# Splitting the second mixer's weights one layer stage earlier and passing both parts through DRAM

## The chip, the cores and the metric

The kernel runs on one core of one Trainium2 chip. The metric is the device time of one execution in microseconds (us); of several executions the median is taken.

The core has a matrix engine (PE, with its weight load shown apart as PEld), a vector engine (DVE), an activation engine (ACT), a general engine (POOL) and a queue processor (SP). In this kernel SP issues every transfer between DRAM and the on-chip memory. Each engine works through its own list of instructions in order; an instruction that waits holds up everything behind it on its engine.

## The reference

Two layers run one after the other on 512 tokens of 1024 channels, in float32:

```
h = RMSNorm(x);  z = h @ W_in
a = sparse attention heads (the 128 best keys of each query, by an indexer)
s = S5 heads (a scan over tokens);  m = SSD heads (chunked)
x = x + concat(a, s, m) @ W_out
x = x + relu(RMSNorm(x) @ W_up)^2 @ W_down
```

The part of a layer up to `W_out` is called the mixer here, the last line the MLP. The indexer chooses keys, so products have to be good to about the last bit of float32.

## The kernel before

**Products.** A float32 matrix is held as two parts: `hi`, rounded to the format that PE multiplies fast (`F32R`), and `lo`, the rest. A product is three matmuls (hi·hi, hi·lo, lo·hi), in `mm3`, whose three calls are L436 to L438.

**Weights.** All weights come as slabs of at most 128 x 512 numbers (256 KB), in the order of use: `W_in` of a layer (40 slabs, of which the first 8, `kv`, have 332 columns), then `W_out` (16), then `W_up` and `W_down` (128). `Slabs.load` brings a slab into one of 3 buffers `wraw` (L159), `Slabs.split` makes `whi` on ACT (L171) and `wlo` on DVE (L172), each with 5 buffers. A new `whi` waits until PE has finished with the slab five before; a new `wraw` waits until DVE has split the slab three before. The program asks for slabs 3 ahead and splits them 1 ahead (`AHEAD`).

**Streams.** A mixer is made of several streams of work: the slices of `W_in` (order for the second layer: kv, xa, qi, z, u5, q, xb), the keys and index scores, the choice of keys (`isc`, `mx`: 16 rounds of MAX and MATCH_REPLACE for each of three blocks), attention, S5, SSD and the products with `W_out`. `merge` lays them side by side by costs and priorities, and a list scheduler then fixes each engine's order at build time. In the first MLP a stream `prepare` builds the second layer's S5 tables on POOL, with small transfers `M<-strip` on SP (L666).

**Around u5.** The S5 input slice `u5` needs the inverse root mean square of each token, `rsp`: three Newton steps on DVE (L299 to L305, tiles `rsi`, `rst`, `rsp`). Then ACT copies the product out of PE's accumulators into `usb` (L1186), which sets the accumulators free. The tile `cv` is the SSD convolution (L834 to L841), `cth` its tanh on ACT, `z` and `xb` other slices.

Of the kernel before, what the change touches and what calls it, by code (L numbers as in the profile page):

```python
# [22 lines left out]
NB = S // P          # token blocks  # L23
KC = D // P          # channel chunks of the trunk
# [8 lines left out]
T5 = 8               # tokens of one S5 chunk  # L33
C5 = S // T5         # S5 chunks
G5 = 16
GBUFS = {"g": 52, "t": 16}
BANKS = {"m": 4, "a": 4}    # PSUM banks: trunk, attention, S5 and SSD
EARLY = 2           # slabs loaded along with x
S5_ON_DVE = True
CONV_ON_ACT = False  # L40
# how the streams of work of a layer's mixers are laid side by side: the order of W_in's slices, the blocks whose
# selections run side by side, the parts of the out projection, which of S5 and SSD waits for the other, each
# stream's pace and delay, and the banks
# [41 lines left out]
WB = (3, 5)    # weight slabs in flight: as loaded, and split  # L85
OUTER = {"tok": True, "chan": True}    # products slab by slab
AHEAD = (3, 1)    # slabs requested and split ahead of the one in use

# columns of the packed per-partition parameters
# [18 lines left out]
# constants  # L108
# [8 lines left out]
# W_in slices: (first column, width), in the host's column order  # L117
# [16 lines left out]

class Slabs:
    """slabs of weight matrices in the order of their use: loaded and split into hi and lo parts some way ahead"""
# [9 lines left out]
    def turn(self, key):  # L146
        """whether the slabs before these have been used up"""
        return self.i == self.starts[key]

    def load(self, upto):  # L150
        for src in self.srcs[len(self.raw):upto]:
            net = self.net
            if len(self.raw) < EARLY:
                t = net.g(name="wraw0")
            else:
                t = net.wp.tile([P, 512], F32, tag="wraw", name=net.nm("wraw"), bufs=WB[0])
# [5 lines left out]
    def split(self, upto):  # L162
        upto = min(upto, len(self.srcs))
        self.load(upto)
        for raw in self.raw[len(self.hl):upto]:
            net = self.net
            nc = net.nc
# [13 lines left out]
    def take(self, n, tiles, outer):  # L181
        """the next n slabs for each of some tiles, as (tile, slab number, hi, lo): slab by slab if outer, else
        tile by tile, and then those to follow are split while the last tile uses these up"""
# [17 lines left out]
class Net:  # L201
    def __init__(self, ctx, tc, a, taps=None):
# [9 lines left out]
        self.sp = e(tc.tile_pool(name="sp", bufs=4))  # L212
        self.pp = {k: e(tc.tile_pool(name=f"p{k}", bufs=n, space=PSUM)) for k, n in BANKS.items()}
        self.uid = 0

# [9 lines left out]
    def h(self, shape=(P, 512), dt=F32, name="h"):  # L225
        """as g, for S5 and SSD"""
        return self.g(shape, dt, name, "h")

    def tt(self, shape=(P, 512), dt=F32, name="t"):
        """as g, for the matrices of S5"""  # L230
        return self.g(shape, dt, name, "t")

    def small(self, n, tag="g"):
        """[P, n] tiles for what one stretch of small instructions needs, cut from one slot"""
# [59 lines left out]
    def rsqrt(self, y, x, n, eng=None):  # L294
        """y = 1/sqrt(x), [P, n] small"""
# [11 lines left out]
    def stt(self, v, out, x, s, y, op0, op1):  # L307
        """out = (x op0 s) op1 y, [P, n] small; GpSimd takes two instructions for it"""
# [7 lines left out]
    def expacc(self, out, x, t, v):  # L316
        """out = exp(x) to about an ulp, [P, n] small"""
# [15 lines left out]
    def sincos(self, c, s, th, t, v):  # L333
        """c, s = cos(th), sin(th), [P, n] small"""
# [14 lines left out]
        self.stt(v, q, q, 1.0, r, ALU.add, ALU.mult)      # sin(th/2)  # L349
# [4 lines left out]
        # cos(th/2) = 1 + w  # L354
# [9 lines left out]
    def norm_chunk(self, c, squares=True):  # L364
        """hi and lo parts of x*g, and the sum of squares over channels (still per partition)"""
# [25 lines left out]
    def token_sums(self, acc, perm=False):  # L391
        """[P, 4]: mean square + eps per token; block b is tokens b*128 + m, or with perm 4m + 3-b"""
# [10 lines left out]
    def bcast_tokens(self, colv, k):  # L403
        """[P, 4] per-token columns -> psum tile [P, 512] with the token's value on every partition"""
# [6 lines left out]
    def add_slabs(self, l):  # L411
        """the weights of a layer, in the order of their use"""
# [9 lines left out]
        self.slabs.add(("in", l), [t for o in out for t in o])  # L422
# [5 lines left out]
        for part in PLAN[l]["out"]:  # L428
            self.slabs.add((part, l), square(a["w_out"][l], rows[part[0]][0], rows[part[-1]][1]))
# [3 lines left out]
    def mm3(self, p, lh, ll, rh, rl, first, last):  # L433
        """p += (lh+ll)^T (rh+rl), without the product of the two low parts (below float32's last bit)"""
# [5 lines left out]
    def gemm_tok(self, ps, xh, xl, slabs, sls):  # L440
        """token-major blocks: psum tile of block i [tok, n] = ps(i), tokens sls[i]; yields (cost, finished tile)"""
# [14 lines left out]
    def gemm_chan(self, ps, slabs, xh, xl):  # L456
        """channel-major tiles of 128 columns of a slice of 256: [chan, tok]; yields (cost, finished tile)"""
# [13 lines left out]
    def s5_small(self):  # L471
        """powers of the discretised state matrix and the input matrices, both layers"""
# [38 lines left out]
        # powers 0..8  # L511
# [17 lines left out]
        # X = (pr; pi), Y = (-pi; pr) on the two halves of the partitions  # L529
# [8 lines left out]
        # m8 and the rotation of one chunk, with the angle's sign turned on the lower half  # L538
# [4 lines left out]
        self.rot = []          # e^{+-i phi 2^k}  # L543
# [22 lines left out]
    def s5_tables(self, l, t):  # L566
        """the matrices of one layer's chunked recurrence, into t"""
# [29 lines left out]
        def outer(v, out, u, w, u2, w2, gs, d0, d1):  # L597
            """out[g, d, h] = u[g, h] w[g, d] + u2[g, h] w2[g, d]"""
# [935 lines left out]
```

## Time and profile before

| | |
|---|---|
| median of three runs | 1359.96 us (1359.14 to 1361.53) |
| span of the profiled execution | 1356.7 us; the median is 3.3 us longer, for what lies around the span |
| PE busy | 1247.9 us (92%), 5852 matmuls |
| DVE busy | 883.2 us (65%) |
| ACT busy | 564.6 us (42%) |
| POOL busy | 161.6 us (12%) |
| transfers | 103.7 MB, 76 GB/s over the span |

The execution has four stages: the first mixer (to about 329 us), the first MLP (to about 731), the second mixer (to about 1018) and the second MLP. The second mixer's first products begin some 20 us before 731, beside the end of the MLP. A matmul's listed duration overlaps that of the next: 128x512 products follow each other every 0.23 us though each is listed with 0.39.

### The profile page before, as it was taken

How to read it: one execution, taken by the hardware profiler on the slowest of the kernel's cores; microseconds unless marked ns; L12 is line 12 of the kernel's file. 1: busy time of each engine (PE TensorE's matmuls, PEld its weight loads, DVE VectorE, ACT ScalarE, POOL GpSimd, SP SyncE). 2: the span in 40 equal slices, each digit the busy share in tenths (PEclk: the TensorE clock that was granted, in tenths of full speed). 3: DMA queues.
4: the chain of work that ended last, by engine and by line, in shares of the span. 5: the costliest groups of instructions: out<-in, count | busy, mean ns of one | idle time of the engine just before them, and what ended most of it. 6: DMA issues, size and time to landing. Idle time of an engine off the chain costs nothing. (4 is left out here: it accounts for less than half of the span.)

```text
span 1356.7 us, 17071 instructions
## 1 busy us (share of the span) xinstructions
PE 1247.9 (92%) x5852; PEld 1013.6 (75%) x5852; DVE 883.2 (65%) x2044; ACT 564.6 (42%) x1160; POOL 161.6 (12%) x301
## 2 busy tenths in 40 slices
PE   6679966879999999999999998978999999999998
PEld 5667854647888877888888897755688888888887
DVE  6899799884844544444466779998575444445443
ACT  4346352563542332423444535656454233242331
POOL 2593268200000221000000000000000000000000
PEclk9789987899999999999999998989999999999999
DMA  6122120001233323323323312100123333333332
GB/s 193 47 78 71 25 68 11 32 1 47 86 95 100 94 83 94 101 96 99 94 84 89 100 31 53 63 16 16 35 83 102 95 99 94 101 94 101 93 108 86
DMA packets 102694, 103.74 MB, mean 76 GB/s; under 512 B 10960, under 2 KB 95696, under 8 KB 102608
## 3 DMA queue, kind: packets, MB, share of 16 engines
q1 hardware_dynamic: 102608, 102.66, 25.1%
q8 instruction: 46, 0.75, 0.2%
q14 instruction: 40, 0.33, 0.1%
HBM read 99.36 MB, written 2.10 MB: 75 GB/s over the span
## 5 line engine op out<-in xcount | busy, mean ns | idle before, releaser
L172 DVE TENSOR_TENSOR wlo<-wraw,whi 128x512 fp32r<-128x512 f32 (+1 forms) x368 | 253.8, 691 | 300.6 <-ACT whi L171 298.4
L171 ACT ACTIVATE whi<-wraw 128x512 fp32r<-128x512 f32 (+1 forms) x368 | 229.0, 624 | 498.5 <-PE pm L437 332.4
L436 PE MATMUL pm<-xh,whi 128*128 128x512 f32 x608 | 239.8, 395 | 2.7 <-ACT usb L1186 1.1
L437 PE MATMUL pm<-xl,whi 128*128 128x512 f32 x608 | 238.5, 393 | 0.0
L438 PE MATMUL pm<-xh,wlo 128*128 128x512 f32 x608 | 238.4, 393 | 0.0
L438 PE MATMUL pm<-uh,wlo 128*128 128x512 f32 x512 | 199.5, 390 | 1.2 <-DVE wlo L172 1.2
L437 PE MATMUL pm<-ul,whi 128*128 128x512 f32 x512 | 199.7, 390 | 0.0
L436 PE MATMUL pm<-uh,whi 128*128 128x512 f32 x512 | 199.6, 390 | 0.0
L436 PEld LDWEIGHTS pm<-xh,whi 128*128 128x128 f32 x608 | 115.2, 190 | 27.6 <-ACT q L1210 1.6
L438 PEld LDWEIGHTS pm<-xh,wlo 128*128 128x128 f32 x608 | 115.1, 189 | 24.4 <-issue 0.3
L437 PEld LDWEIGHTS pm<-xl,whi 128*128 128x128 f32 x608 | 115.3, 190 | 23.1 <-DVE xl L372 0.2
L438 PEld LDWEIGHTS pm<-uh,wlo 128*128 128x128 f32 x512 | 96.2, 188 | 21.7 <-DVE wlo L172 1.6
L436 PE MATMUL pm<-whi,xh 128*128 128x512 f32 (+2 forms) x240 | 94.1, 395 | 19.8 <-ACT xh L370 12.4
L437 PEld LDWEIGHTS pm<-ul,whi 128*128 128x128 f32 x512 | 96.2, 188 | 20.3 <-issue 0.4
L436 PEld LDWEIGHTS pm<-uh,whi 128*128 128x128 f32 x512 | 96.2, 188 | 19.9 <-issue 0.2
L437 PE MATMUL pm<-wlo,xh 128*128 128x512 f32 (+2 forms) x240 | 92.5, 386 | 2.3 <-DVE wlo L172 2.3
L438 PE MATMUL pm<-whi,xl 128*128 128x512 f32 (+2 forms) x240 | 92.2, 388 | 1.5 <-DVE xl L372 1.4
L436 PEld LDWEIGHTS pm<-whi,xh 128*128 128x128 f32 x240 | 55.9, 234 | 27.1 <-ACT xh L370 12.8
L437 PEld LDWEIGHTS pm<-wlo,xh 128*128 128x128 f32 x240 | 56.3, 235 | 7.6 <-DVE wlo L172 3.4
L438 PEld LDWEIGHTS pm<-whi,xl 128*128 128x128 f32 x240 | 55.7, 234 | 7.1 <-DVE xl L372 2.5
L1384 DVE SCALAR_TENSOR_TENSOR ur<-pm,ur 128x512 f32<-128x512 f32 x64 | 44.0, 687 | 25.5 <-ACT ur L1381 25.5
L1392 DVE TENSOR_TENSOR sq<-pm,r2b 128x512 f32<-128x512 f32 x64 | 44.2, 690 | 23.2 <-PE pm L438 23.2
(349 smaller groups left out, 1915.2 us busy)
## 6 DMA issues: line engine op xcount, KB each, us to landing
wraw<-in_w_up_dram SPq DMA_DIRECT2D x128, 256.0 KB, 2.7
wraw<-in_w_down_dram SPq DMA_DIRECT2D x128, 256.0 KB, 2.7
wraw<-in_w_in_dram SPq DMA_DIRECT2D x64, 256.0 KB, 2.7
wraw<-in_w_out_dram SPq DMA_DIRECT2D x32, 256.0 KB, 2.7
wraw<-in_w_in_dram SPq DMA_DIRECT2D x16, 166.0 KB, 2.3
x<-in_xT_dram SPq DMA_DIRECT2D x8, 256.0 KB, 5.9
out_dram<-x SPq DMA_DIRECT2D x8, 256.0 KB, 2.0
s5bc<-in_s5bc_dram SPq DMA_DIRECT2D x4, 256.0 KB, 4.7
```

The source lines that it names most:

```text
L171: nc.scalar.activation(hi, raw, AF.Copy)
L172: nc.vector.tensor_tensor(lo, raw, hi.bitcast(F32), ALU.subtract)
L436: nc.tensor.matmul(p, lh, rh, start=first, stop=False)
L437: nc.tensor.matmul(p, lh, rl, start=False, stop=False)
L438: nc.tensor.matmul(p, ll, rh, start=False, stop=last)
L1384: v.scalar_tensor_tensor(r, p, 0.0, r, ALU.max, ALU.mult)
L1392: v.tensor_tensor(t, d[1], rb, ALU.mult)
```

## The change

The 56 slabs of the second layer's `W_in` and `W_out` are no longer split by `Slabs.split`. A new stream `stage` runs beside the first MLP and the table stream: for each slab it loads the raw numbers (`sraw`), makes `shi` on ACT and `slo` on DVE, and stores both in DRAM (`st`). In the second mixer `Slabs.load` brings both parts straight into `whi` and `wlo`, by two transfers. The first layer and both MLPs are split as before.

```
+class Staged:
+    def __init__(self, src):
+        self.src, self.shape = src, src.shape
+        self.k, self.n = src.shape[0] // P, src.shape[1]
+        self.parts = None
...
     def load(self, upto):
         for src in self.srcs[len(self.raw):upto]:
             net = self.net
+            if isinstance(src, Staged):
+                hl = [net.wp.tile([P, 512], F32R, tag=t, name=net.nm(t), bufs=WB[1])[:, :src.k * src.n]
+                      for t in ("whi", "wlo")]
+                for t, d in zip(hl, src.parts):
+                    net.nc.sync.dma_start(t.bitcast(F32), d)
+                self.raw.append([t.rearrange("p (k n) -> p k n", k=src.k) for t in hl])
+                continue
...
     def split(self, upto):
...
+            if isinstance(raw, list):
+                self.hl.append(tuple(raw))
+                continue
...
+    def stage(self):
+        nc = self.nc
+        yield 6.0
+        for st in [t for t in self.slabs.srcs if isinstance(t, Staged)]:
+            w = st.k * st.n
+            raw, hi, lo = self.g(name="sraw")[:, :w], self.g(dt=F32R, name="shi")[:, :w], self.g(dt=F32R, name="slo")[:, :w]
+            nc.sync.dma_start(raw.rearrange("p (k n) -> p k n", k=st.k), st.src.rearrange("(k p) n -> p k n", p=P))
+            nc.scalar.activation(hi, raw, AF.Copy)
+            nc.vector.tensor_tensor(lo, raw, hi.bitcast(F32), ALU.subtract)
+            st.parts = [self.dp.tile([P, w], F32, tag=self.nm("st"), name=self.nm("st"), bufs=1) for _ in range(2)]
+            for d, t in zip(st.parts, (hi, lo)):
+                nc.sync.dma_start(d, t.bitcast(F32))
+            yield 5.3
...
             if l + 1 < L:
                 streams.append((self.prepare(l + 1), 0.0))
+                streams.append((self.stage(), 0.0))
```

Line numbers in the rows of the changed kernel are its own: L1437 is the store of `stage`, L167 the load of a staged part, L1099 and L1100 are MAX and MATCH_REPLACE, L321 to L326 the steps of `rsp`, L860 and L864 belong to `cv`.

On DVE, in the second mixer, where the steps of `rsp` for the slice u5 stand (`isc` of 128x256 belongs to the key choice of the first block that has one, `isc<-irl` to the last block's index scores). Before:

```order
L299 TENSOR_SCALAR rsi_1845_7697<-ms_7694 128x4
L172 TENSOR_TENSOR wlo_7744<-wraw_7644,whi_7743 128x512
L837 SCALAR_TENSOR_TENSOR cv_7561<-xa_7112,hconvw,cv_7561 128x509
L300 TENSOR_SCALAR rsp_7696<-rsi_1845_7697 128x4
L172 TENSOR_TENSOR wlo_7973<-wraw_7677,whi_7972 128x512
L303 TENSOR_TENSOR rst_1846_7700<-rsp_7696 128x4
L841 SCALAR_TENSOR_TENSOR cv_7561<-cth_7566,cv_7561 128x512
L1066 SCALAR_TENSOR_TENSOR isc_7426<-irl_7572,wd_6683,isc_7426 128x512
L304 SCALAR_TENSOR_TENSOR rst_1846_7700<-rst_1846_7700,ms_7694 128x4
L172 TENSOR_TENSOR wlo_7997<-wraw_7741,whi_7996 128x512
L1066 SCALAR_TENSOR_TENSOR isc_7426<-irl_7614,wd_6683,isc_7426 128x512
L305 SCALAR_TENSOR_TENSOR rsp_7696<-rst_1846_7700,rsp_7696 128x4
```

The same place after the change:

```order
L320 TENSOR_SCALAR rsi_2210_8205<-ms_8202 128x4
L1100 MATCH_REPLACE isc_7790<-mx_2266_8514,isc_7790 128x256
L860 SCALAR_TENSOR_TENSOR cv_8075<-xa_7652,hconvw,cv_8075 128x509
L321 TENSOR_SCALAR rsp_8204<-rsi_2210_8205 128x4
L1099 MAX mx_2269_8533<-isc_7790 128x8
L324 TENSOR_TENSOR rst_2211_8208<-rsp_8204 128x4
L1099 MAX mx_2434_9146<-isc_7870 128x8
L864 SCALAR_TENSOR_TENSOR cv_8075<-cth_8080,cv_8075 128x512
L1089 SCALAR_TENSOR_TENSOR isc_7950<-irl_8086,wd_7247,isc_7950 128x512
L325 SCALAR_TENSOR_TENSOR rst_2211_8208<-rst_2211_8208,ms_8202 128x4
L1100 MATCH_REPLACE isc_7790<-mx_2269_8533,isc_7790 128x256
L1089 SCALAR_TENSOR_TENSOR isc_7950<-irl_8126,wd_7247,isc_7950 128x512
```

The four `wlo` between the first and the last step of `rsp` are gone (the fourth stood just below the rows shown), and rounds of the key choice, which stood later before, have moved up between the steps.

On SP, in the first MLP, loads of its own weights before the change:

```order
L159 DMA wraw_4166<-in_w_down_dram 128x2x256
L159 DMA wraw_4190<-in_w_down_dram 128x2x256
L159 DMA wraw_4210<-in_w_up_dram 128x2x256
L159 DMA wraw_4228<-in_w_up_dram 128x2x256
L159 DMA wraw_4246<-in_w_up_dram 128x2x256
```

A place of the first MLP after the change:

```order
L1432 DMA sraw_4142<-in_w_in_dram 128x2x256
L176 DMA wraw_4252<-in_w_down_dram 128x2x256
L176 DMA wraw_4270<-in_w_down_dram 128x2x256
L1437 DMA st_4148<-shi_4143 128x512
L1437 DMA st_4149<-slo_4144 128x512
L1432 DMA sraw_4188<-in_w_in_dram 128x2x256
L176 DMA wraw_4298<-in_w_down_dram 128x2x256
L176 DMA wraw_4322<-in_w_down_dram 128x2x256
```

After every two loads of the MLP's own weights SP now has two stores, which wait for ACT and DVE, and one load for the next staged slab.

On SP, where the second mixer's weights begin to be loaded, after the change (before, each slab is one row `wraw<-in_w_in_dram` there):

```order
L176 DMA wraw_7148<-in_w_down_dram 128x2x256
L167 DMA whi_7168<-st_3656 128x332
L167 DMA wlo_7169<-st_3657 128x332
L176 DMA wraw_9920<-in_w_up_dram 128x2x256
L176 DMA wraw_9952<-in_w_up_dram 128x2x256
L167 DMA whi_7188<-st_3717 128x332
L167 DMA wlo_7189<-st_3718 128x332
L176 DMA wraw_9984<-in_w_up_dram 128x2x256
```

Each slab is now two rows, and the first three slabs of the second MLP, whose `wraw` buffers the mixer no longer uses, are loaded some 290 us before they are needed.

## Rows read from the trace of the kernel before

**Rows 1.** Stages: us; PE, PEld, DVE, ACT, POOL busy (count); clock; DMA share; GB/s.

```profile
329.00:731.00 402.00, 398.86 (x1828) 331.44 (x1827) 213.62 (x333) 148.46 (x252) 21.51 (x34) 1.00 0.31 95
731.00:1018.00 287.00, 257.74 (x1294) 203.13 (x1293) 229.56 (x658) 152.37 (x359) 0.52 (x1) 0.95 0.17 50
```

**Rows 2.** Groups of instructions, 725 to 1020 us: the splits of the second mixer.

```profile
L172 DVE TENSOR_TENSOR wlo<-wraw,whi 128x512 fp32r<-128x512 f32 x56 | 38.2, 686 | 11.5 <-ACT whi L171 10.9 <-PE pm L438 0.2
...
L171 ACT ACTIVATE whi<-wraw 128x512 fp32r<-128x512 f32 x56 | 35.3, 632 | 57.7 <-PE pm L437 23.6 <-PE pm L438 22.8 <-issue 6.0
```

**Rows 3.** PE's waits, 715 to 830 us (us in total, times, longest).

```profile
PE pm L436 <- ACT usb L1186: 5.2, 1, 5.2
PE pm L436 <- ACT whi L171: 1.4, 2, 0.7
...
PE pm L437 <- DVE wlo L172: 0.6, 2, 0.4
```

**Rows 4.** DVE in order of time (start, us; idle before and releaser).

```profile
802.47 0.16 DVE L299 TENSOR_SCALAR rsi<-ms 128x4 int32<-128x4 int32 x1
805.15 0.69 DVE L172 TENSOR_TENSOR wlo<-wraw,whi 128x512 fp32r<-128x512 f32 x1 [2.52 <-ACT whi L171]
805.76 0.74 DVE L837 SCALAR_TENSOR_TENSOR cv<-xa,hconvw,cv 128x509 f32<-128x509 f32 x1
...
810.04 0.69 DVE L841 SCALAR_TENSOR_TENSOR cv<-cth,cv 128x512 f32<-128x512 f32 x1 [2.55 <-ACT cth L839]
...
814.14 0.42 DVE L1076 MAX8 mx<-isc 128x8 f32<-128x256 f32 x1
...
816.47 0.14 DVE L305 SCALAR_TENSOR_TENSOR rsp<-rst,rsp 128x4 f32<-128x4 f32 x1
```

**Rows 5.** ACT in order of time, 795 to 830 us.

```profile
808.86 0.63 ACT L171 ACTIVATE whi<-wraw 128x512 fp32r<-128x512 f32 x1 [2.16 <-PE pm L438]
809.40 0.61 ACT L839 ACTIVATE cth<-cv 128x512 f32<-128x512 f32 x1
```

**Rows 6.** PE in order of time: the last u5 product, and the next.

```profile
811.70 0.40 PE L438 MATMUL pm<-whi,xl 128*128 128x256 f32 x1
817.32 0.80 PE L436 MATMUL pm<-whi,xh 128*128 128x512 f32 x1 [5.23 <-ACT usb L1186]
```

**Rows 7.** Stretches of 4 us around that gap (PE busy; granted clock).

```profile
800.00:804.00 4.00, 4.00 (x17) 0.80 0.00 0
...
816.00:820.00 4.00, 2.68 (x9) 0.50 0.10 35
820.00:824.00 4.00, 4.00 (x26) 0.64 0.00 0
```

**Rows 8.** The chain of waits that ended last, splits on it from 829 us.

```profile
848.05 0.69 DVE wlo L172
...
872.02 0.52 ACT whi L171
...
885.83 0.60 DVE wlo L172
```

**Rows 9.** SP in order of time, 470 to 560 us, in the first MLP.

```profile
470.93 29.59 SPq L159 DMA_DIRECT2D wraw<-in_w_down_dram  x11
502.24 16.37 SPq L666 DMA_DIRECT2D M<-strip  x24
```

**Rows 10.** PE's waits for DVE, 330 to 735 us (total, times, longest).

```profile
PE pm L438 <- DVE wlo L172: 1.2, 1, 1.2
```

**Rows 11.** Transfers: issue on SP (ns), then issues by kind with time to landing.

```profile
L159 SPq DMA_DIRECT2D wraw<-in_w_up_dram x128: 367/368/957, 333.9 to 1288.1; - x128
```

**Rows 12.** The page's transfers by kind (KB each, median us to landing).

```profile
wraw<-in_w_in_dram SPq DMA_DIRECT2D x64, 256.0 KB, 2.7
...
out_dram<-x SPq DMA_DIRECT2D x8, 256.0 KB, 2.0
```

**Rows 13.** Two microseconds of the opening load of x (DMA share; GB/s).

```profile
8.00:10.00 2.00, 0.16 (x1) 0.16 (x1) 0.68 (x2) 1.30 (x3) 2.00 (x9) 1.00 1.05 399
```

More of the change, by code (lines that the diff above doesn't have):

```diff
@@ L212, in __init__ @@
         self.sp = e(tc.tile_pool(name="sp", bufs=4))
+        self.dp = e(tc.tile_pool(name="dp", bufs=2, space=bass.MemoryType.DRAM))
         self.pp = {k: e(tc.tile_pool(name=f"p{k}", bufs=n, space=PSUM)) for k, n in BANKS.items()}
@@ L421, in add_slabs @@
             out[:2] = [[t for j in range(4) for t in (kv[2 * j], kv[2 * j + 1], x[j])]]
-        self.slabs.add(("in", l), [t for o in out for t in o])
+        out = [t for o in out for t in o]
+        self.slabs.add(("in", l), [Staged(t) for t in out] if l else out)
         def square(w, r0, r1):
@@ L428, in add_slabs @@
         for part in PLAN[l]["out"]:
-            self.slabs.add((part, l), square(a["w_out"][l], rows[part[0]][0], rows[part[-1]][1]))
+            out = square(a["w_out"][l], rows[part[0]][0], rows[part[-1]][1])
+            self.slabs.add((part, l), [Staged(t) for t in out] if l else out)
         self.slabs.add(("mlp", l), [t for q in range(0, FF, D)
```

## The prediction

> **What bounds the kernel now.** I read the busy times by stage first [rows 1]. In the first MLP PE is busy 398.86 of 402 us while DVE and ACT are busy 213.62 and 148.46 and the transfers take .31 of their engines: PE bounds it and all others have room. In the second mixer PE is busy 257.74 of 287 us and DVE 229.56, so about 29 us of the stage are not PE's, and neither is DVE the bound by its sum alone. What a lighter DVE is worth there depends on where PE stands still. I therefore looked at the groups for the work that leaves [rows 2], at PE's waits [rows 3], then at DVE, ACT and PE in order of time round the longest of these waits [rows 4 to 6] with the clock beside it [rows 7], and at the chain of waits for the rest [rows 8]. For what is added I read SP in the first MLP [rows 9], what PE lost there [rows 10], and the prices of transfers [rows 11 to 13].
>
> **What leaves the second mixer.** 56 `wlo` on DVE (38.2 us busy; one is listed with 0.69 but the next begins 0.61 us behind it, at 805.76 after 805.15 [rows 4]) and 56 `whi` on ACT (35.3 us) [rows 2]. That is 17% of DVE's busy time in the stage, but only what stands between two pieces of PE work is a gain:
>
> *Before u5.* Between 715 and 830 us PE waited directly for splits only four times: `whi` 1.4 us and `wlo` 0.6 us [rows 3]. Both go: **−2.0**.
>
> *The u5 gap.* PE starts its last u5 product at 811.70 and its next at 817.32, having stood 5.23 us for ACT's `usb` [rows 6]; that is the 5.2 of [rows 3]. `usb` needs the last `rsp` step, which starts on DVE at 816.47 and ends at 816.6; the first step starts at 802.47 [rows 4]. So the chain lasts 14.1 us. In it lie 2.52 us in which DVE waited for a `whi`, 2.55 in which it waited for `cth`, and four `wlo` of about 0.60, 2.4 together. The wait for `cth` falls too: ACT ran `cth` at 809.40 only because the `whi` at 808.86 ahead of it had stood 2.16 us until PE freed its buffer [rows 5]. Against that, the change puts ten rounds of MAX and MATCH_REPLACE between the steps, where five stood before (the order of the program, counted to the last step); one takes about 0.4 us [rows 4], so +2.0. The chain becomes 14.1 − 2.5 − 2.5 − 2.4 + 2.0 = 8.7 us and ends near 811.2; with the 0.7 us from there to PE's start, PE may go on at 811.9, and its last product before ends at 812.1. Nearly all of the 5.2 would go; I take **−4.5**, because a transfer or `cv` may be late next. The ends: −1 if the waits for ACT stay in another form, −5.2 if all goes.
>
> *The clock.* Around the gap the granted clock was .80 at 800 to 804 while PE was busy all 4 us, then .50 at 816 to 820 with PE busy 2.68, and .64 at 820 to 824 with PE busy 4.00 [rows 7]; .50 is the 1.2 GHz level, 1.00 that of 2.4 GHz. At the level of 2.4 GHz the busy time of the last two stretches would have needed 2.68 × .5 + 4.00 × .64 = 3.9 us instead of 6.68: 2.8 us lost. If PE doesn't stand, this loss may go. But ACT's copies out of PE's accumulators pace the same stretch, and the clock was already low at 800 before any gap; between 0 and −2.8 I take **−0.5**.
>
> The Trainium skill, "TensorE: Matmul & The Clock Gate", Part 1, says that the clock is gated by PE's recent activity, so that standing idle drops it to the lower level. The half clock right behind the 5.23 us agrees [rows 6, 7]; the .80 beside a busy PE does not follow from it. By that rule alone the whole 2.8 us would come back, by the rows I count a part.
>
> *After 829 us* the chain that ended last runs for a part over DVE, and six `wlo` lie on it, from 848.05 to 885.83, with 3.74 us in all, and two `whi` of 0.52 [rows 8], 4.8 us. A piece that leaves the chain gives back its length only until the next path ends last, and rounds of the key choice can fill its place only where they were not due anyway. I count four fifths: **−3.9**, with bounds 0 and −4.8. A later stand of PE, near 905 us, has no split ahead of it, and I leave it.
>
> **What is added to the first MLP.** The same 56 splits: 35 us for ACT (148 busy of 402) and 38 us for DVE (214 of 402) [rows 1, 2]. Both would be at most 63% busy, behind a PE that is at 99%; the splits of the MLP run a few slabs ahead, limited by their five buffers, so half a microsecond on either engine is taken from that lead. Cost 0; without the lead it would be one `wlo`, 0.6, per staged slab, 34 us.
>
> SP has 168 more instructions there, 56 loads and 112 stores, at .37 us [rows 11] 62 us of issuing. That is no load on SP by itself; the question is what they hold up. A store waits for `shi` or `slo`, and behind it stand the MLP's own loads. How sensitive PE is to a held SP can be read: 24 strips of M held SP for 16.37 us, with no weight load among them [rows 9], and PE's whole wait for `wlo` in the stage was 1.2 us [rows 10]. The buffers therefore cover some 14 us. Ahead of a pair of stores stand two `wraw` loads, which themselves wait for buffers, so ACT and DVE have about 5.4 us (two slabs at SP's 2.7 [rows 9]) for the load of 2.7 us [rows 12] and the two splits. Round the strips two stores and a load are added to a cover that is just used up: I take **+2.0** in the whole stage, from 0 to +4.
>
> The transfers: 14 MB read and 28 MB written in about 297 us are 141 GB/s beside the 95 of [rows 1], 236 in all; at 8 to 10 us the trace has 399 [rows 13]. It fits.
>
> **What is added to the second mixer.** Two loads for one, 28 MB instead of 14. PE takes a slab of `qi` in some 2.07 us (nine spans of 0.23), 0.52 MB in that time being 250 GB/s, under the 399 [rows 13]. The load is now issued when PE frees the fifth buffer back; then four slabs, over 7 us, remain for a landing of 2.7 us [rows 12], or some 4 with two issues and other traffic. This removes the engine from the path, but it also makes SP wait for PE where it waited for DVE. I take **+1.0**, from 0 to +4. Behind a waiting load stand only small parameter loads and the next parts.
>
> **Sum.** −2.0 − 4.5 − 0.5 − 3.9 + 2.0 + 1.0 = −7.9 us. From the span of 1356.7 that is 1348.8; the median of the runs is 3.3 us over the span, so 1352.1. The terms' ends on one side or the other give 1347 to 1358 as this case's own range.
>
> **Rivals.**
>
> *SP is held in the first MLP (slower).* If the pace does not hide the staged slab, SP's cycle is its issue .37, the landing 2.7, `shi` .63, a store .37, `slo` .69, a store .37 and two loads .74 [rows 2, 11, 12], together 5.9 us. SP's own pace is 29.59 us for eleven loads [rows 9], 2.7 a slab and 5.4 for the two. Over 56 staged slabs 0.5 us each are 28; some 14 are covered, 14 stay, and with the mixer's gains of 8 kept the time is about 1366. It decides from the point at which a staged slab holds SP longer than PE needs for two slabs of the MLP. Against it: the load is put two paced loads ahead of its stores, which takes the 2.7 us out of the sum.
>
> By the Trainium skill, "DMA: Bandwidth & Descriptors", Anatomy of one DMA, a transfer's wait for a semaphore is served by the issuing sequencer before dispatch, so waiting stores do hold the loads behind them; and a write to DRAM has the heaviest receipt. The first agrees with [rows 9]; no row shows the second, the stores of the output landing in 2.0 us against 2.7 for loads [rows 12].
>
> *The gains are eaten (same).* The gap of u5 is filled by the added rounds of the key choice, or its place is taken by `cv` and ACT; the pieces on the chain come back at 905 us, and +3 to +5 of transfers remain: −2.0 − 1 − 1 + 4 = 0, 1360.
>
> *A larger gain.* DVE's rounds of the key choice are what the later part of the mixer waits for, and all 38 us that leave let them end earlier; with the whole clock loss back and no cost in the first MLP it would be −2.0 − 5.2 − 2.8 − 4.8 = −14.8, about 1345, and the prefetched slabs at the start of the second MLP can add a little.
>
> That the change doesn't do what it says is out: the order has none of the `wlo` in the second mixer, and SP's list is 224 longer, four for each of 56 slabs.
>
> **Chances.** The forecast .58; larger gain .12; eaten .16; SP held .14. Within 0.2%, 2.7 us, which is about what a measurement of this kernel can tell from no change, lie the eaten case and the upper edge of the forecast; a part of the slow case ends there too. Faster .69, same .17, slower .14. The range leaves out the slow case above 1363 and a bit of the large gain below 1343.
>
> **What would show it.** Right: no PE wait for `usb` over 1 us near 812; the mixer's span shorter by about 10 us and the first MLP's within 3 us of before; `sraw` landing in about 3 us. Wrong: PE waits of MLP for `wlo` or `whi` spread over all of the first MLP (SP held), or PE waits in the mixer for DMA `whi` or `wlo` (loads late); or PE's gap at u5 as before with another releaser.

## The result, and the profile after

The changed kernel takes 1371.3 us (median of 1366.5 to 1374.3), the kernel before 1359.6 in the same comparison: 0.81% slower, a ratio of 1.0081 with a 95% interval of 1.0058 to 1.0104. I had forecast 1352.1.

The stage windows of the changed kernel, which answer to [rows 1], show the first MLP with more work and a PE that now stands still:

```profile
329.00:731.00 402.00, 383.43 (x1685) 311.29 (x1684) 226.68 (x353) 167.64 (x288) 17.50 (x29) 0.98 0.62 194
731.00:1018.00 287.00, 262.86 (x1368) 211.87 (x1367) 207.95 (x622) 125.96 (x314) 0.52 (x1) 0.97 0.32 101
```

PE has 1685 matmuls in the same 402 us instead of 1828: the stage is not over at 731. Its end can be read from the last residual sum of the first MLP on DVE (`x<-x,sq`), and the end of the second mixer from its last one (`x<-x,pm`). In order of time on DVE, kernel before:

```profile
716.92 0.69 DVE L1393 TENSOR_TENSOR x<-x,sq 128x512 f32<-128x512 f32 x1
...
1012.77 0.69 DVE L1354 TENSOR_TENSOR x<-x,pm 128x512 f32<-128x512 f32 x1 [2.00 <-PE pm L438]
```

The same two rows of the changed kernel:

```profile
738.80 0.69 DVE L1416 TENSOR_TENSOR x<-x,sq 128x512 f32<-128x512 f32 x1
...
1024.73 0.69 DVE L1377 TENSOR_TENSOR x<-x,pm 128x512 f32<-128x512 f32 x1 [2.25 <-PE pm L461]
```

From one row to the other the second mixer takes 285.9 instead of 295.9 us, 9.9 less. But it begins 21.9 us later. Taken from the first mixer's last sum (end at 357.3 before, 354.8 after), the first MLP takes 384.7 instead of 360.3 us: 24.4 more. By stages the profiled executions differ by −2.5, +24.4, −9.9 and +0.1, in sum by the 12.0 us between the spans of 1356.7 and 1368.7. The −2.5 lies in the first mixer, which the change doesn't touch (see the end).

The two windows of the first MLP hold the same 1608 matmuls, before and after:

```profile
357.34:717.61 360.27, 357.13 (x1608) 294.57 (x1607) 184.02 (x278) 128.62 (x219) 21.51 (x34) 1.00 0.31 95
354.79:739.49 384.70, 366.13 (x1608) 297.15 (x1607) 212.15 (x329) 156.54 (x270) 17.50 (x29) 0.98 0.64 201
```

PE stands 18.6 us instead of 3.1, which is 15.4 more, and is busy 9.0 us longer for the same products, at a granted clock of .98 instead of 1.00.

PE's waits in the first MLP (330 to 740 us; us in total, times, longest), to be laid beside [rows 10]:

```profile
PE pm L459 <- DVE ur L1407: 12.9, 6, 4.8
PE s5st L676 <- POOL CA L629: 3.2, 2, 1.6
PE pm L459 <- DVE sq L1415: 2.5, 4, 1.4
```

No wait for `whi` or `wlo` is left: the MLP's weights are there in time. PE waits for `ur` and `sq`, the copies that take a finished product out of its accumulators, 15.4 us in all. Behind the two longest waits the granted clock falls as well (stretches of 20 us; the last three numbers are clock, DMA share and GB/s):

```profile
580.00:600.00 20.00, 14.46 (x56) 10.91 (x55) 10.09 (x16) 9.40 (x16) 0.00 (x0) 0.90 0.65 208
600.00:620.00 20.00, 20.00 (x83) 16.14 (x83) 8.61 (x14) 5.25 (x9) 0.00 (x0) 0.93 0.55 174
680.00:700.00 20.00, 14.35 (x51) 10.56 (x50) 9.74 (x15) 9.04 (x16) 0.00 (x0) 0.87 0.67 215
```

What happens at such a wait is seen round 592 us, on three engines. SP in order of time:

```profile
591.40 0.34 SPq L1437 DMA_DIRECT2D st<-slo  x1
591.79 0.45 SPq L1432 DMA_DIRECT2D sraw<-in_w_in_dram  x1
```

ACT:

```profile
592.13 0.63 ACT L191 ACTIVATE whi<-wraw 128x512 fp32r<-128x512 f32 x1 [1.57 <-issue]
595.10 0.63 ACT L1433 ACTIVATE shi<-sraw 128x512 fp32r<-128x512 f32 x1 [2.34 <-DMA sraw<-in_w_in_dram]
595.64 0.58 ACT L1404 ACTIVATE ur<-pm 128x512 f32<-128x512 f32 x1
```

PE:

```profile
591.88 0.39 PE L461 MATMUL pm<-uh,wlo 128*128 128x512 f32 x1
597.11 1.88 PE L459 MATMUL pm<-uh,whi 128*128 128x512 f32 x3 [4.84 <-DVE ur L1407]
```

PE finishes a product at 592.3 and needs the copies that empty its accumulators: ACT's `ur`, and behind it DVE's `ur`, which the row names. ACT could do its own at 592.8, but its next instruction is `shi`, which waits 2.34 us for the raw staged slab. That slab was requested only at 591.79, because its load stands in SP's list behind the store of the slab before, and this store waited for `slo`. So a staged slab goes round a ring: load, `shi`, `slo`, store, next load. And ACT's list has `shi` straight ahead of the copy that PE waits for. All six waits for `ur` lie behind a `shi` that had stood for `sraw`, for 0.9 to 4.7 us. DVE's list has the same form: the `sq` of the longest such wait (1.41 us, before 552.67) stands directly behind a `slo` that had waited 1.38 us for its `shi`.

ACT's own waits from 357 to 740 us show what it stood for (us in total, times, longest):

```profile
ACT shi L1433 <- DMA sraw<-in_w_out_dram: 43.9, 14, 4.7
ACT shi L1433 <- DMA sraw<-in_w_in_dram: 38.9, 30, 2.7
ACT whi L191 <- DMA wraw<-in_w_up_dram: 7.3, 8, 1.7
```

It stood 82.8 us for staged slabs and under 8 for the MLP's own, less than the 12.4 us of the kernel before (357 to 718 us). SP's list did not hold the MLP's own loads back to any effect here.

The ring's period is read from the tile view of `sraw` (min/median/max ns on SP, first and last issue):

```profile
L1432 SPq DMA_DIRECT2D sraw<-in_w_out_dram x16: 399/442/503, 610.6 to 706.5; - x16
```

15 steps in 95.9 us are 6.4 us each, PE's own waits included. Where nothing is held, as in e1_ahead below, the same 15 steps take 82.2 us, 5.5 each: that is the pace at which the stage was laid beside the MLP. Early in the stage the changed kernel keeps it too: 23 steps from 368.3 to 496.4 us, 5.6 each. Then the strips hold SP, and the next `sraw` is issued at 517.5.

In the second mixer, PE's waits (735 to 1030 us) have neither `usb` nor `whi` nor `wlo` in them, where [rows 3] had all three. The largest that are left:

```profile
PE ssds L906 <- DVE CT L871: 4.8, 1, 4.8
PE pTp L1136 <- ACT pe L1128: 3.0, 3, 2.4
PE kTp L1043 <- ACT khi L1037: 2.9, 1, 2.9
```

### The profile page after: what moved, and what is told of

It reads as the page before. It is cut to its first block, busy times and chain, and to the rows that moved or that the text cites. A ratio compares the mean times of both kernels' runs of the same rounds, so it can differ in the third digit from the quotient of the medians.

```text
span 1368.7 us, 17369 instructions
## 1 busy us (share of the span) xinstructions
PE 1249.4 (91%) x5852; PEld 1010.4 (74%) x5852; DVE 884.6 (65%) x2044; ACT 563.0 (41%) x1160; POOL 161.3 (12%) x301
## 4 chain that ended last, share of the span: by engine, by line
PE 70%; DVE 16%; ACT 6%; DMA 4%; issue 2%; SPq 0%; POOL 0%; ACTq 0%; DVEq 0%
PE pm L459 20%; PE pm L460 20%; PE pm L461 20%; PE po L1141 2%; DMA sraw<-in_w_in_dram 2%; DMA sraw<-in_w_out_dram 2%; PE pTp L1136 1%; DVE isc L1100 1%; DVE mx L1099 1%; DVE wlo L192 1%; ACT pe L1121 1%; DVE pe L1120 1%; DVE isc L1089 1%; DVE cv L860 1%; PE hTp L1059 1%
## 5 line engine op out<-in xcount | busy, mean ns | idle before, releaser
L192 DVE TENSOR_TENSOR wlo<-wraw,whi 128x512 fp32r<-128x512 f32 (+1 forms) x312 | 217.4, 700 | 224.6 <-ACT whi L191 222.8
L191 ACT ACTIVATE whi<-wraw 128x512 fp32r<-128x512 f32 (+1 forms) x312 | 194.3, 625 | 358.8 <-PE pm L460 239.8
L459 PE MATMUL pm<-uh,whi 128*128 128x512 f32 x512 | 201.9, 396 | 11.7 <-DVE ur L1407 11.2
L1434 DVE TENSOR_TENSOR slo<-sraw,shi 128x512 fp32r<-128x512 f32 (+1 forms) x56 | 37.3, 666 | 78.0 <-ACT shi L1433 74.8
L1433 ACT ACTIVATE shi<-sraw 128x512 fp32r<-128x512 f32 (+1 forms) x56 | 34.0, 608 | 82.9 <-DMA sraw<-in_w_out_dram 43.9
```

What stands on the lines that cost most here:

```text
L191: nc.scalar.activation(hi, raw, AF.Copy)
L192: nc.vector.tensor_tensor(lo, raw, hi.bitcast(F32), ALU.subtract)
L459: nc.tensor.matmul(p, lh, rh, start=first, stop=False)
L1433: nc.scalar.activation(hi, raw, AF.Copy)
L1434: nc.vector.tensor_tensor(lo, raw, hi.bitcast(F32), ALU.subtract)
```

## The experiments

The theory after this reading, called RING or ORDER in the expectations: the loss comes of the ring, whose period under load is about as long as the stage's step. Rivals: the traffic as such (VOLUME, LOAD or TRAFFIC), and the 73 us of added work on ACT and DVE (WORK). All experiments start from the changed kernel.

**e1_ahead.** The raw slab of the next step is requested before the present one is split.

```
+        raws = [fetch(sts[0])]
+        for n, st in enumerate(sts):
+            if n + 1 < len(sts):
+                raws.append(fetch(sts[n + 1]))
             ... (split raws[n], store)
```

> The raw slab of the next stage step is requested before the present one is split, so no sraw stands behind the stores of the slab before it. Theory ORDER (a ring: sraw behind the stores of the slab before, its shi on ACT ahead of the copy ur that frees PE's accumulators, the stores behind slo): PE's waits for ur and sq in the first MLP fall from 15.4 us to under 4, that stage gets about 20 us shorter, time about 1351. Rival VOLUME (the transfers' 200 GB/s make loads land late): nothing changes, about 1371. Rival WORK (73 us more on ACT and DVE stand ahead of the drains): about 1371 too.

Measured 1355.5 us, a ratio of 0.9976 (0.9964 to 0.9989) to the kernel before. The waits for `ur` and `sq` are gone; PE's waits from 330 to 735 us are

```profile
PE s5st L676 <- POOL CA L629: 5.0, 2, 3.8
PE pm L461 <- DVE wlo L192: 0.3, 1, 0.3
```

and the first MLP takes 363.8 us. The tile view has `sraw` in an even step again:

```profile
L1433 SPq DMA_DIRECT2D sraw<-in_w_out_dram x16: 385/463/961, 597.4 to 679.6; - x16
```

With the same bytes and the same splits, order alone gives back 21 of 24 us. WORK is out. The time is 4 us above the 1351 expected; the stage table below says where. Of the 3.5 us by which the first MLP is still longer than before, 2.1 are PE standing: its wait for the S5 tables (`s5st`, 5.0 us above) was 1.9 in the kernel before. It is 4.9 in e11_ahead_small as well, so the stores' bytes are not its cause.

**e2_pool_stores.** The stores go into POOL's queue.

```
-                nc.sync.dma_start(d, t.bitcast(F32))
+                nc.gpsimd.dma_start(d, t.bitcast(F32))
```

> The stores of the staged parts are issued by POOL instead of SP; same bytes, same splits. ORDER: sraw is no longer held by a store, PE's waits for ur go, about 1351, unless POOL's own table work gets late behind waiting stores (then PE waits for POOL, 2 to 6 us more). VOLUME and WORK: about 1371.

Measured 1374.3. The waits for `ur` are gone here too, but POOL, held for 358.6 us by stores that wait (161.7 at the longest; 330 to 740 us), is late with the S5 tables, and by far more than the 2 to 6 us that I had allowed:

```profile
PE s5st L676 <- POOL CA L629: 20.1, 2, 19.0
PE s5B L641 <- POOL BPp L629: 2.9, 1, 2.9
```

**e3_small_stores.** All stores stay in their places, but write 8 columns; the second mixer loads the first slab's parts for all slabs, so its numbers are not the weights.

```
+            full = self.first.setdefault(w, [])
...
+            c = 8 if full else w
             for d, t in zip(st.parts, (hi, lo)):
-                nc.sync.dma_start(d, t.bitcast(F32))
+                nc.sync.dma_start(d[:, :c], t.bitcast(F32)[:, :c])
+            full.append(st.parts)
+            st.parts = full[0]
```

> All 112 stores stay in place and still wait for shi and slo, but except for the first slab of each width they write 8 columns only, and the second mixer loads the first slab's parts for all slabs (so its numbers are not the weights). The volume of the first MLP falls from about 200 to 130 GB/s. ORDER: the ring stays, sraw lands a little sooner, about 1366 to 1371. VOLUME: the loss goes, about 1350.

Measured 1347.7 (0.9916 to 0.9958 of before). This went against ORDER as I had put it: the order is unchanged, and yet the waits for `ur` are gone. The bytes matter, then, and what they change for the ring is the landing of the raw slab. Transfers of 640 to 700 us (KB each, median us from issue to landing), first the changed kernel:

```profile
wraw<-in_w_up_dram SPq DMA_DIRECT2D x9, 256.0 KB, 3.8
...
sraw<-in_w_out_dram SPq DMA_DIRECT2D x9, 256.0 KB, 3.7
```

then this run:

```profile
sraw<-in_w_out_dram SPq DMA_DIRECT2D x7, 256.0 KB, 2.9
```

From 400 to 640 us, in stretches of 40 us, the medians are 3.2 to 4.1 in the changed kernel and 2.9 to 3.1 in this run. An estimate from these rows: with landing L, the ring needs L, then `shi` and `slo` of about 0.7 each, then a store's issue of 0.4, which is 5.5 us at 3.7 and 4.7 at 2.9. A step is 5.5 us. At 3.7 the ring has no slack at all, and each `wraw` between its members that waits for its buffer adds to it; at 2.9 it has 0.8 us a step to make a delay good. So both must come together: the closed order, and the bytes that lengthen it.

**e5_free.** Only the first slab of each width is staged, and the second mixer loads those for all slabs (its numbers are not the weights).

```
+            if w in first:
+                st.parts = first[w]
+                continue
```

> Only the first slab of each width is staged, and the second mixer loads those two slabs' parts for all 56 slabs (its numbers are not the weights): the second half of the change without its price in the first MLP. All theories: the first MLP is as before, and the time is 1360 less the gain of the mixer read from the two traces (9.9 us): about 1348 to 1350. If the mixer gains less when the MLP ahead of it is not late, 1355 or more.

Measured 1346.8, 11.7 us below the kernel before in the same comparison (0.990 to 0.9941). That is the second half of the change without its price in the first MLP. It is not all the mixer's gain: in this run's trace the second mixer is 9.5 us shorter than before, as in the changed kernel's, and the first mixer, which nothing touches, another 2.0.

**e6_pace6.** A longer step of the stage.

```
-            yield 5.3
+            yield 6.0
```

> The stage takes a step every 6.0 cost units instead of 5.3: one staged slab per some 6.2 us instead of 5.4, same order within a step. Theory RING (sraw issue to the next sraw issue takes 5.2 to 6.5 us, because two stores of 256 KB go into the queue right ahead of each sraw and it lands 3.0 to 4.7 us after its issue; that is as long as the step, so a delay is never made up): with the longer step the ring can catch up, PE's waits for ur and sq fall below 5 us, time 1352 to 1360. Rival LOAD (the traffic as such slows the stage): 12% less traffic per time takes off 12% of 24 us, about 1368.

Measured 1362.9: most of the loss is gone, but not as far as RING said. Until 700 us no wait for `ur` or `sq` is left. The last staged slabs then come at the MLP's very end, and there the link returns, by DVE's list this time:

```profile
716.39 0.42 PE L459 MATMUL pm<-whi,xh 128*128 128x332 f32 x1 [0.67 <-DVE sq L1415]
726.37 0.64 PE L459 MATMUL pm<-whi,xh 128*128 128x332 f32 x1 [5.54 <-DVE sq L1415]
```

The `sq` that frees the accumulators stands on DVE behind a `slo`, and this behind the `shi` on ACT that waits for its slab:

```profile
724.36 0.63 ACT L1433 ACTIVATE shi<-sraw 128x512 fp32r<-128x512 f32 x1 [4.34 <-DMA sraw<-in_w_out_dram]
725.02 0.69 DVE L1434 TENSOR_TENSOR slo<-sraw,shi 128x512 fp32r<-128x512 f32 x1 [4.28 <-ACT shi L1433]
725.63 0.68 DVE L1415 TENSOR_TENSOR sq<-pm,r2b 128x512 f32<-128x512 f32 x1
```

**e7_pause.** The old step, with a pause of three steps behind the strips.

```
-        for st in [t for t in self.slabs.srcs if isinstance(t, Staged)]:
+        for n, st in enumerate([t for t in self.slabs.srcs if isinstance(t, Staged)]):
...
-            yield 5.3
+            yield 5.3 + 5.3 * 3 * (n == 25)
```

> The step stays at 5.3, but after the 26th slab, where the 24 strip transfers of the S5 tables hold SP, the stage pauses for three steps. RING with the strips as the trigger: the ring is in time again behind the strips, most of PE's waits behind 540 us go, 1352 to 1360. RING without a trigger (any ring period over 5.4 us piles up): waits come back in the last 100 us of the stage, 1362 to 1368. LOAD: 1371.

Measured 1369.1. From 540 to 660 us PE waits no more, then the waits come back, from 663 us on:

```profile
675.24 0.50 PE L459 MATMUL pm<-uh,whi 128*128 128x512 f32 x1 [2.39 <-DVE ur L1407]
687.78 0.79 PE L459 MATMUL pm<-uh,whi 128*128 128x512 f32 x1 [3.46 <-DVE ur L1407]
```

This is RING without a trigger, at a time just over its 1362 to 1368. The strips are then not the whole cause: they are where the ring first falls behind, but after a pause of three steps it falls behind again, with landings of 3.9 us (600 to 640) and 4.1 (640 to 700). No run leaves the strips out.

**e8_ahead_late.** As e1_ahead, and each slab's stores are issued one step later.

```
...
-            for d, t in zip(st.parts, (hi, lo)):
+            for d, t in late:
                 nc.sync.dma_start(d, t.bitcast(F32))
+            late = list(zip(st.parts, (hi, lo)))
```

> Raw slabs requested one step ahead, as in the run before, and each slab's stores issued one step later, when their parts are long done, so that no store holds SP either. RING: as with the early request alone, 1352 to 1356. If what that run left (some 3.5 us of the first MLP) was SP held by stores, 1350; if it is the traffic, no better than 1355.

Measured 1357.1; the first MLP takes 364.0 us, as in e1_ahead. Waiting stores were not what that run had left.

**e9_act_stores.** The stores go into ACT's queue.

```
-                nc.sync.dma_start(d, t.bitcast(F32))
+                nc.scalar.dma_start(d, t.bitcast(F32))
```

> The stores go into ACT's queue: sraw on SP neither waits for nor stands behind a store, but ACT itself waits for slo (about 0.7 us) at the second store of each slab. RING: sraw is early, PE's waits for ur fall below 5 us, 1352 to 1362, where ACT's own waits take up to 0.7 us of a drain. LOAD: 1371 or more.

Measured 1356.9 (0.9963 to 0.9989). The ring is open, the waits for `ur` are gone with all the bytes still written, and PE has one wait of 3.2 us for `whi`, which I take for the price of ACT's own waiting (it stood 27.3 us in all behind stores that waited for `slo`); the first MLP takes 367.0 us.

**e10_in_only.** As e1_ahead, but only the 40 slabs of `W_in` are staged.

```
-            self.slabs.add((part, l), [Staged(t) for t in out] if l else out)
+            self.slabs.add((part, l), out)
...
-            yield 5.3
+            yield 7.3
```

> Only the 40 slabs of W_in are staged, one per 7.3 cost units, with the early request; the 16 of W_out are split in the second mixer as before. Traffic in the first MLP falls by 28%. RING: no waits for ur in the first MLP, the mixer keeps the u5 gain (no 5.2 us wait) and the direct waits, 7 us of its 10, so 1352 to 1355; below the early request alone (1355.5) only if the traffic of that run cost the rest. If the splits of W_out in the mixer's later part cost nothing, 1349.

Measured 1356.0 (0.9974 to 0.9994). The first MLP pays nothing (359.5 us), and the second mixer takes 292.4, only 3.5 less than before where I had expected 7.

**e11_ahead_small.** e1_ahead and e3_small_stores together; the second mixer's numbers are again not the weights.

```
+                raws.append(fetch(sts[n + 1]))
...
+                nc.sync.dma_start(d[:, :c], t.bitcast(F32)[:, :c])
```

> Early request and small stores together (8 columns after the first slab of each width, the mixer loads the first slab's parts, so its numbers are not the weights). It tells what the 8 us are by which the early request with full stores (1355.5) stands above small stores in the old order (1347.7). TRAFFIC (the stores' bytes cost the stage even where no one waits in the ring): 1347. CLOCK or ORDER (that kernel's own order or granted clock, .95 in its second mixer against .98): 1353 to 1356.

Measured 1354.4 (1350.0 to 1358.6). Once the ring is open, taking the bytes away as well changes about 1 us, within the spread, and the first MLP is as long as in e1_ahead (364.5 against 363.8): TRAFFIC is out as a cost of its own. What stays unexplained is that this run lies 6.7 us over e3_small_stores, which has the old order; the two traces differ by 8.2, of which 3.1 lie in the first mixer, 3.0 in the first MLP and 2.1 in the second mixer.

**e12_ahead_pace6.** e1_ahead with a step of 5.9.

```
-            yield 5.3
+            yield 5.9
```

> Early request with a step of 5.9 cost units instead of 5.3. RING: broken already, so no change beyond 2 us, 1353 to 1356. TRAFFIC: 11% less of it per time, 1 us better at most.

Measured 1351.1, a ratio of 0.9955 (0.9937 to 0.9972) to the kernel before: the fastest version with the whole computation. It is 2 us below what I expected. The first MLP takes 363.4 us, the same as e1_ahead, so the traces do not show that the slower step did it.

**e13_pool_split.** The changed kernel with `shi` and `slo` on POOL.

```
-            nc.scalar.activation(hi, raw, AF.Copy)
-            nc.vector.tensor_tensor(lo, raw, hi.bitcast(F32), ALU.subtract)
+            nc.gpsimd.tensor_copy(hi, raw)
+            nc.gpsimd.tensor_tensor(lo, raw, hi.bitcast(F32), ALU.subtract)
```

> The change as it was, but shi and slo are made on POOL (about 1.2 us each there by the tables' 128x512 instructions) instead of ACT and DVE: nothing of the stage stands ahead of the copies that free PE's accumulators any more, while SP's list keeps the stores between the loads, and the ring gets longer (landing 3.3, two splits 2.4, stores .7, near 6.8 us a step). HEAD (the loss comes only from shi standing ahead of ur and xh on ACT): PE's waits for ur go and nothing takes their place, 1346 to 1354. SP (the late ring also holds the MLP's own loads, which stand in the same list): PE waits for whi or wlo by late wraw instead, 56 steps of 6.8 against 5.4 us minus the buffers' cover, 1375 to 1430.

Measured 1406.7. Neither theory had the largest part: POOL's tables stand behind splits that waited for `sraw` (347.7 us in all), and PE waits for the tables 40 us (330 to 790 us):

```profile
PE s5st L676 <- POOL CA L629: 27.4, 3, 23.2
PE s5B L641 <- POOL BPp L629: 12.7, 2, 10.9
PE pm L459 <- DVE ur L1407: 6.1, 4, 2.9
```

Waits for `ur` are left though no `shi` stands on ACT. In its place ACT waits for the MLP's own loads, far more than in the changed kernel; here from 600 to 765 us:

```profile
ACT whi L191 <- DMA wraw<-in_w_down_dram: 28.7, 11, 5.3
ACT whi L191 <- DMA wraw<-in_w_up_dram: 18.9, 7, 4.3
```

So a ring that is late enough seems to reach the drains by SP's list too. How much of the changed kernel's loss would be left if only ACT's and DVE's order were mended, this run doesn't tell.

The stages of all profiled executions, in us, each from the end of one stage's last sum to that of the next:

| | first mixer | first MLP | second mixer | second MLP | span, this execution | median of runs |
|---|---|---|---|---|---|---|
| before | 357.3 | 360.3 | 295.9 | 343.2 | 1356.7 | 1359.6 |
| changed | 354.8 | 384.7 | 285.9 | 343.3 | 1368.7 | 1371.3 |
| e1_ahead | 359.1 | 363.8 | 290.3 | 343.3 | 1356.5 | 1355.5 |
| e2_pool_stores | 353.5 | 387.2 | 285.9 | 343.3 | 1369.9 | 1374.3 |
| e3_small_stores | 354.5 | 361.5 | 285.1 | 343.2 | 1344.4 | 1347.7 |
| e5_free | 355.3 | 360.2 | 286.4 | 343.2 | 1345.0 | 1346.8 |
| e6_pace6 | 358.0 | 372.6 | 286.4 | 343.2 | 1360.2 | 1362.9 |
| e7_pause | 356.9 | 381.8 | 283.0 | 343.2 | 1364.9 | 1369.1 |
| e8_ahead_late | 357.1 | 364.0 | 290.3 | 343.3 | 1354.6 | 1357.1 |
| e9_act_stores | 358.9 | 367.0 | 284.6 | 343.3 | 1353.8 | 1356.9 |
| e10_in_only | 357.2 | 359.5 | 292.4 | 343.3 | 1352.4 | 1356.0 |
| e11_ahead_small | 357.6 | 364.5 | 287.2 | 343.3 | 1352.6 | 1354.4 |
| e12_ahead_pace6 | 360.5 | 363.4 | 284.5 | 343.3 | 1351.6 | 1351.1 |
| e13_pool_split | 352.7 | 425.7 | 286.6 | 343.3 | 1408.3 | 1406.7 |

In e6_pace6 and e7_pause some of the second mixer's first products lie ahead of the boundary (21 and 25, in e12_ahead_pace6 four), so these two stages are read as a sum. Each row is one execution: that of e1_ahead was the slowest of its ten, that of e3_small_stores the fastest of its ten.

## Why the prediction was wrong

**The step that failed** is the term of +2.0 (0 to +4) for SP in the first MLP; it measured +24.4. Two steps under it were wrong. That ACT and DVE have about 5.4 us for the load of 2.7 and the two splits counted the way out but not the way back: the next `sraw` stands behind the stores, so a step isn't 2.7 and two splits inside 5.4, but a ring of landing, `shi`, `slo` and store inside 5.5. And its landing wasn't the 2.7 of [rows 12] but 3.7, amid the stage's own stores (2.9 where these are small). That the transfers fit was true of the average (201 GB/s in the first MLP, of 399) and said nothing of a landing in a ring. e3 shows that a landing of 2.9 is enough to heal it, e1 and e9 that opening the order is, with every byte still written; e6 that a longer step helps; e7 that the strips, which I had taken for the main risk, are not the whole cause.

**The cover** of 14 us from [rows 9, 10] was that of the weight buffers, and it did hold: PE never waited for `whi` or `wlo` in the first MLP. What had no cover were the drains. I costed ACT's and DVE's added splits at nothing, as taken from that lead, but `shi` is in one list with ACT's `ur`, and `slo` with DVE's `ur` and `sq`, and PE stood 15.4 us for these. The working asked how busy ACT is (63% at most), not what stands right behind a waiting instruction on it.

**The slower rival** had the right direction and most of the cycle, with a price of 14 us and a time of 1366, but not the place where it costs. It let the MLP's own loads come late, and its sign, waits for `wlo` or `whi` over all of the stage, did not come. It had .14 of the chance, because I let the two paced loads ahead of the stores take the landing out of the sum. They pace SP, but don't shorten the way from one `sraw` to the next. The clock adds to it: of the 24.4 us, 9.0 are PE's busy time for the same products, with .90, .93 and .87 granted in the stretches shown. No term of the sum had this.

**The range.** The lower and upper ends of the terms, as they are given, add up to −14.8 and +5.0, which is 1345 to 1365 and not 1347 to 1358; four fifths of 4.8 are 3.8, not 3.9. Neither slip brings 1371.3 into reach.

**The second mixer's sum** was met by luck: −2.0 − 4.5 − 0.5 − 3.9 + 1.0 is −9.9, and the traces have −9.9, but made up of other terms. The window of the stage, from last sum to last sum (PE busy with the count first, the granted clock third from the end), before:

```profile
717.61:1013.46 295.85, 266.59 (x1356) 212.49 (x1354) 234.06 (x672) 155.47 (x365) 0.52 (x1) 0.95 0.19 54
```

the changed kernel, and then e1_ahead:

```profile
739.49:1025.42 285.93, 261.79 (x1356) 210.34 (x1354) 206.16 (x621) 125.87 (x314) 0.52 (x1) 0.97 0.32 100
```

```profile
722.88:1013.22 290.34, 265.92 (x1356) 212.46 (x1354) 206.20 (x621) 125.96 (x314) 0.53 (x1) 0.95 0.32 99
```

Span less busy time, PE stands 29.3 us before, 24.1 in the changed kernel and 24.4 in e1_ahead. The waits gave some 5 us, not the 9.4 of −2.0 − 4.5 − 3.9 + 1.0. The waits for `usb` (5.2) and for splits (2.0) did go, and no wait for a late load came. The waits for `CT`, `pe` and `cv` later in the mixer also fell, from 6.0, 5.4 and 3.0 to 4.8, 3.0 and 2.4, in sum by 4.2; but other waits, new or longer, took some 6 us back, such as the 2.9 us for `khi`, which the kernel before does not have. No run shows why they came. The other 4.8 us are PE's busy time for the same 1356 matmuls, at a clock of .97 instead of .95: I had put 0.5 there, with a bound of 2.8. This part isn't sure to belong to the change, since e1_ahead, with the same waits, doesn't have it (265.9 busy at .95).

The u5 gap itself went as worked out. Its chain on DVE, from the first to the last of these rows, takes 8.1 us, against 14.1 before and 8.7 forecast:

```profile
826.93 0.16 DVE L320 TENSOR_SCALAR rsi<-ms 128x4 int32<-128x4 int32 x1
...
834.91 0.15 DVE L326 SCALAR_TENSOR_TENSOR rsp<-rst,rsp 128x4 f32<-128x4 f32 x1
```

PE has no wait for `usb` there, and the granted clock is 1.00 from 830 to 846 us where [rows 7] have .50 and .64.

**What stays open**: why the granted clock of the second mixer is .95 in e1_ahead and e8_ahead_late and .97 or .98 in the changed kernel, e9_act_stores and e12_ahead_pace6, with 290.3 us against 284.5 to 285.9. It is the largest difference of stages between the trace of e12_ahead_pace6 (1351.1 by median) and those of the first two (1355.5 and 1357.1), whose first MLPs are as long. With one trace of each kernel, it isn't shown whether it belongs to the kernel or to the execution. The Trainium skill, "TensorE: Matmul & The Clock Gate", Part 1, ties the clock to PE's recent activity; the stage's waits, which are all but the same in these runs, don't show the difference.

## What to carry to other kernels

When a side job is laid beside a stage that one engine bounds, follow its own cycle round through every list it stands in (load, split, store, next load), and compare that period, with the landing that it will have under its own traffic, with the pace of the stage; busy shares show nothing of it. Then look at what stands directly behind each of its waiting instructions: here it was not the weights, which had five buffers, but the copies that free the accumulators. One early request turned a loss of 0.8% into a gain of 0.24%; with a slightly slower step beside it the gain was 0.45%, though the traces don't show that the step did the rest.

## What the runs showed of the hardware

The first mixer has the same instructions in the same order on PE, ACT, DVE and SP in all these kernels, and yet took 352.7 to 360.5 us in the profiled executions of the table, at a granted clock of .90 to .92. Only POOL differs: it works on the S5 tables in this stage, with 180 instructions in e2_pool_stores and e13_pool_split, the two shortest, and 266 to 271 in the others, whose own range is 354.5 to 360.5. A single span of this kernel thus carries some 3 to 4 us either way from there; the stages are better compared one by one.

A staged load of 256 KB, issued right behind two stores of 256 KB, landed in 3.7 us in the median (640 to 700 us), against 2.9 where those stores were small, though the stretch moved only 215 GB/s, about half of the 399 of [rows 13]. In e1_ahead, at 203 GB/s with the load ahead of the stores, it was

```profile
sraw<-in_w_out_dram SPq DMA_DIRECT2D x7, 256.0 KB, 3.1
```

but the place in the queue does not settle it: in the same stretch e6_pace6, with the load right behind the stores, has 3.2 (207 GB/s), and from 600 to 640 us the landing is 3.9 in e1_ahead, 4.1 in e9_act_stores, whose stores are in another queue, and 4.1 in the changed kernel. What sets a landing between 3 and 4 us beside full stores, these runs leave open. By the Trainium skill, "DMA: Bandwidth & Descriptors", Anatomy of one DMA, a transfer's wait for a semaphore is served by the issuing sequencer before dispatch; the `sraw` at 591.79, right behind a store that had waited for `slo`, agrees.

On POOL the split of a 128x512 slab took 0.61 us for `shi` and 1.29 for `slo` (medians of e13_pool_split), against 0.63 for `shi` on ACT and 0.69 for `slo` on DVE. Stores issued from POOL (e2_pool_stores) held up its other work while they waited for `shi`, and PE stood up to 19.0 us at one place for it.
